# Nearest-neighbour upsampling: the first store cut into four transfers, and the closing waits moved to GpSimd

## The chip, the cores and the metric

The kernel runs on one core of one Trainium2 chip. The metric is the device time of one execution in microseconds (us), lower being better. Each comparison below was timed in rounds on one chip, with the kernel before in the same rounds. Kernels are compared only within the same rounds. A profiled execution comes with each; its "span", from the first to the last instruction, is about 1.8 us shorter than the device time. Unless said otherwise, times inside an execution count from the start of the span.

## The reference

The input is float32 of shape 16 x 64 x 64 x 64, and every element is repeated twice in height and twice in width. The loops of the reference come down to this:

```python
for i in range(new_h):
    for j in range(new_w):
        result[:, :, i, j] = x[:, :, i // 2, j // 2]
```

So 16.8 MB are read and 67.1 MB written, and nothing is computed.

## The kernel before

Four blocks of input are loaded, 4.2 MB each. VectorE and ScalarE expand rows inside SBUF, 9/16 and 7/16 of each piece, and SyncE issues all loads and stores on one queue. One input row is 256 B, and it becomes 1 KB of output. The two halves of one buffer take turns for eight stores of 32 rows for each partition ("small"), then two larger buffers for four stores of 64 rows ("large").

```python
blocks = [(1, M4, 0), (1, M4, 2), (1, M4, 3), (4, M4 // 4, 1)]   # the last load has rows of 8 KB, the others of 32 KB
for n, (j, m, slot) in enumerate(blocks):
    ...
    nc.sync.dma_start(out=..., in_=...)                            # all four loads, at the start

def store(part, r0, k, at):
    xp, first, m = part
    kv = k * 9 // 16
    ...
    nc.vector.tensor_copy(out=u[:, :kv], in_=expanded(xp[:, r0 : r0 + kv, :]))
    nc.scalar.copy(out=u[:, kv:], in_=expanded(xp[:, r0 + kv : r0 + k, :]))
    dst = of[first : first + P * m, :].rearrange("(p m) w -> p m w", p=P)
    nc.sync.dma_start(out=dst[:, r0 : r0 + k, :], in_=u)

for n, (q, r0) in enumerate(small):
    store(q, r0, 32, WX + n % 2 * (WU // 2))
for n, (q, r0) in enumerate(large):
    store(q, r0, 64, (0, WX)[n % 2])
```

A hook that the kernel already had issues the first load ahead of the opening barrier. Behind the kernel's own code stands a closing part that the framework adds. A semaphore is a counter on which transfers and engines report that they are done. SyncE waits for all eight DMA completion semaphores (called lanes here) and for VectorE and ScalarE. A barrier over all engines follows, GpSimd clears the semaphores, and a second barrier follows. In a barrier, GpSimd gathers one signal from each other engine and then releases them. "Drain" is an instruction in an engine's queue that here carries some of these waits and signals.

Of the kernel before, what the change touches and what calls it, by code (L numbers as in the profile page):

```python
# [1 line left out]

# [4 lines left out]



EARLY = 1  # L10


def begin_before_barrier(nc):



    blocks = nc.main_func.blocks
    main, body = blocks[0], blocks[1]
    sp = mybir.EngineType.SP
    loads = [i for i in body.instructions if i.engine == sp][:EARLY]  # L20
    for load in loads:
        assert isinstance(load, mybir.InstDMACopy), type(load)
        assert not (load.sync_info and load.sync_info.on_wait)
    names = [i.name for i in loads]
    body.instructions = [i for i in body.instructions if i.name not in names]
    kept = list(main.instructions)
    at = next(
        n
        for n, i in enumerate(kept)
        if i.engine == sp and isinstance(i, mybir.InstDrain)  # L30
    )
    kept[at:at] = loads
    main.instructions = kept


@with_exitstack
def kernel(
    ctx: ExitStack,
    tc: tile.TileContext,
    x: bass.AP,  # L40
    scale_factor: int,
    out: bass.AP,
):
    nc = tc.nc
    nc.at_finalize(begin_before_barrier)
    P = nc.NUM_PARTITIONS
    s = int(scale_factor)
    B, C, H, W = x.shape
    R = B * C * H
    fdt = x.dtype  # L50



    WX = R // P * W
    WU = 16384
    mem_pool = ctx.enter_context(tc.tile_pool(name="mem", bufs=1))
    mem = mem_pool.tile([P, WX + WU], fdt, name="mem")



    M4 = R // (4 * P)
    blocks = [(1, M4, 0), (1, M4, 2), (1, M4, 3), (4, M4 // 4, 1)]
    WB = M4 * W
    assert M4 * P * 4 == R and 2 * WB == WU

    xf = x.rearrange("b c h w -> (b c h) w")
    of = out.rearrange("b c (h hd) w -> (b c h) (hd w)", hd=s)

    parts = []
    for n, (j, m, slot) in enumerate(blocks):  # L70
        first = n * P * M4
        xt = mem[:, slot * WB : (slot + 1) * WB].rearrange(
            "p (j m w) -> p j m w", j=j, m=m
        )
        nc.sync.dma_start(
            out=xt.rearrange("p j m w -> p j (m w)"),
            in_=xf[first : first + P * M4, :].rearrange(
                "(j p m) w -> p j (m w)", j=j, p=P
            ),
        )  # L80
        parts.append([(xt[:, jj], first + jj * P * m, m) for jj in range(j)])

    def expanded(rows):
        return rows.unsqueeze(2).unsqueeze(4).to_broadcast(
            [P, rows.shape[1], s, W, s]
        )

    def store(part, r0, k, at):

        xp, first, m = part  # L90
        kv = k * 9 // 16
        u = mem[:, at : at + k * s * W * s].rearrange(
            "p (k a w b) -> p k a w b", k=k, a=s, w=W
        )
        nc.vector.tensor_copy(out=u[:, :kv], in_=expanded(xp[:, r0 : r0 + kv, :]))  # L95
        nc.scalar.copy(out=u[:, kv:], in_=expanded(xp[:, r0 + kv : r0 + k, :]))  # L96
        dst = of[first : first + P * m, :].rearrange("(p m) w -> p m w", p=P)
        nc.sync.dma_start(out=dst[:, r0 : r0 + k, :], in_=u)



    small = [(q, r0) for n in (0, 3) for q in parts[n] for r0 in range(0, q[2], 32)]
    large = [(q, r0) for n in (1, 2) for q in parts[n] for r0 in range(0, q[2], 64)]
    for n, (q, r0) in enumerate(small):
        store(q, r0, 32, WX + n % 2 * (WU // 2))
    for n, (q, r0) in enumerate(large):
        store(q, r0, 64, (0, WX)[n % 2])


# [1 line left out]
_INS = ['x', 'scale_factor']  # L111
_OUTS = [((16, 64, 128, 128), 'float32')]

_NUMBERS = {'scale_factor': 2}


# [26 lines left out]
```

## Time and profile before

| what | before |
|---|---|
| device time, median of 3 runs | 199.46 us |
| span of the profiled run | 197.7 us |
| first data packet starts, last one ends | 1.01 us, 196.58 us |
| last store landed, to the end of the span | 196.90 us, 0.81 us |
| VectorE, ScalarE busy | 20%, 26% |

These are lines of the page of the kernel before. The digits of the DMA row give the busy share of the 16 DMA engines in tenths, in 40 equal slices of the span. A packet is what one DMA engine moves at a time: 4 to 64 KB of data, or 4 bytes for a semaphore. In the last part the columns are the tensors, the issuing engine, the count, KB each (the page gives none for the four large stores) and the median us from issue to landing.

```profile
span 197.7 us, 116 instructions
DVE 40.2 (20%) x12; ACT 51.3 (26%) x13; POOL 0.2 (0%) x4
...
DMA  8999999999999999999999999999999999999994
...
DMA packets 2688, 83.89 MB, mean 424 GB/s; under 512 B 256, under 2 KB 256, under 8 KB 256
...
q1 hardware_dynamic: 2688, 83.89, 98.9%
...
out_dram<-mem SPq DMA_DIRECT2D x8, 4096.0 KB, 16.1
mem<-in_x_dram SPq DMA_DIRECT2D x4, 4096.0 KB, 25.8
out_dram<-mem SPq DMA_DIRECT2D x4, 32.3
```

The DMA row is full except for its first and last slice, so only three things can shorten this kernel: what stands ahead of the data, what stands behind it, and waste inside the full row.

The chain that ended last, in order of time (start us, us, what), starts so:

```profile
0.00 12.25 DMA mem<-in_x_dram
...
12.27 6.27 ACT mem L96 x2
...
18.56 43.03 DMA out_dram<-mem
```

ScalarE's 6.27 us seem to be on the critical path, but they are not: the other loads are moving all the while, as the DMA row shows. The 43.03 us run from the issue of the second store, at 18.56 us, to its landing at 61.58. The first store was issued at 15.5 us and landed at 51.9, for it stood behind the loads. The landings in the trace say so directly; this is computed from the semaphore records (us from the span's start, then the gaps):

```
loads        12.25  21.94  31.65  42.19                       gaps         9.69  9.71  10.54
small stores 51.90  61.58  71.24  80.92  90.61 100.28 ...     gaps  9.71   9.68  9.66 ...
large stores 138.98 158.31 177.60 196.90                      gaps 19.33  19.33 19.29  19.30
```

Everything lands every 9.7 us for 4.2 MB, except that the fourth load took 10.54 us.

The closing line of the kernel before, by engine queue and operation (count, then durations in ns as minimum, median and maximum, then first and last start in us):

```profile
L138 SPq EVENT_SEMAPHORE  x7: 17/28/28, 165.0 to 197.7; - x7
L138 POOLq EVENT_SEMAPHORE  x4: 17/17/17, 197.1 to 197.6; - x4
...
L138 SPq DRAIN  x3: 7/7/7, 197.0 to 197.3; - x3
...
L138 POOLq EVENT_SEMAPHORE_RANGE_CLEAR  x1: 93/93/93, 197.3 to 197.3; - x1
```

All four of GpSimd's semaphore instructions for the barriers stand behind the last landing at 196.90 us. So do both barriers, and none of it is hidden by data.

### The profile page before, as it was taken

What the parts mean: (1) busy time and instruction counts of PE and PEld (TensorE: products, weight loads), DVE (VectorE), ACT (ScalarE), POOL (GpSimd) and SP (SyncE); (2) the same over time, 40 slices, a digit from 0 to 9 for tenths busy, and PEclk for the clock granted to TensorE, in tenths of its full rate; (3) what the DMA queues carried; (4) which work ended last, traced back from release to release, by engine and by line L of the source; (5) the groups of instructions that cost most, each with busy time, mean ns of one, the idle gap of its engine ahead of it and who ended that gap; (6) DMA issues with size and microseconds to landing.
All of it is one profiled execution on the core that took longest, in us unless ns stands there. A gap on an engine that the chain in (4) does not pass through costs nothing.

```text
span 197.7 us, 116 instructions
## 1 busy us (share of the span) xinstructions
DVE 40.2 (20%) x12; ACT 51.3 (26%) x13; POOL 0.2 (0%) x4
## 2 busy tenths in 40 slices
DVE  0055000000405059505050007200810090000000
ACT  2057000000415150606069207400830092000000
POOL 0000000000000000000000000000000000000000
DMA  8999999999999999999999999999999999999994
GB/s 318 424 424 424 438 464 383 424 413 424 424 424 424 444 444 451 451 424 438 424 424 424 424 424 424 464 477 491 451 451 424 424 424 424 424 424 424 424 424 212
DMA packets 2688, 83.89 MB, mean 424 GB/s; under 512 B 256, under 2 KB 256, under 8 KB 256
## 3 DMA queue, kind: packets, MB, share of 16 engines
q1 hardware_dynamic: 2688, 83.89, 98.9%
HBM read 16.78 MB, written 67.11 MB: 424 GB/s over the span
## 4 chain that ended last, share of the span: by engine, by line
DMA 69%; ACT 14%; issue 0%; ACTq 0%
DMA out_dram<-mem 63%; ACT mem L96 14%; DMA mem<-in_x_dram 6%; ACTq L96 0%
## 5 line engine op out<-in xcount | busy, mean ns | idle before, releaser
L96 ACT COPY mem<-mem 128x3584 f32<-128x3584 f32 (+1 forms) x12 | 50.0, 4174 | 112.5 <-DMA out_dram<-mem 102.2
L95 DVE COPY mem<-mem 128x4608 f32<-128x4608 f32 (+1 forms) x12 | 40.2, 3359 | 123.1 <-DMA out_dram<-mem 110.8
L96 ACT ACT_TABLE_LOAD x1 | 1.3, 1283 | 0.8 <-PEq L124 0.8
L124 POOL MEMSET const-bfloat16-1.0<- 128x1 bf16 x1 | 0.1, 102 | 0.0
L124 POOL MEMSET const-uint8-127<- 128x1 uint8 x1 | 0.1, 102 | 0.0
L124 POOL MEMSET const-float32-0.0<- 128x1 f32 x1 | 0.1, 99 | 0.2 <-issue 0.2
L124 POOL MEMSET const-float32-1.0<- 128x1 f32 x1 | 0.1, 99 | 0.0
## 6 DMA issues: line engine op xcount, KB each, us to landing
out_dram<-mem SPq DMA_DIRECT2D x8, 4096.0 KB, 16.1
mem<-in_x_dram SPq DMA_DIRECT2D x4, 4096.0 KB, 25.8
out_dram<-mem SPq DMA_DIRECT2D x4, 32.3
```

The source lines that it names most:

```text
L95: nc.vector.tensor_copy(out=u[:, :kv], in_=expanded(xp[:, r0 : r0 + kv, :]))
L96: nc.scalar.copy(out=u[:, kv:], in_=expanded(xp[:, r0 + kv : r0 + k, :]))
L124: nc = _bacc.Bacc("TRN2", target_bir_lowering=False, num_devices=1)
```

## The change

One intent is to give the closing waits to GpSimd, which clears the semaphores itself. The first barrier, and the gather of the second, can then run while the last stores still move. After the last landing only a wait, the clear and the release remain. The wait for the last store is placed so that it stands alone and last.

The other intent, as far as the code tells, is to let the first store start with small pieces: 4, 4, 8 and 16 rows, of 4, 4, 8 and 16 KB for each partition. The first three need VectorE's copy alone.

```diff
+def close_on_gpsimd(nc):
+    ...
+    waits = sorted(wait.sync_info.on_wait, key=lambda w: w.id != last)
+    mine = [i for i in end if i.engine == pool]
+    ...
+    d0, gather0, release0, d1, clear, d2, gather1, release1 = mine
+    landed = mybir.InstDrain(name=wait.name, engine=pool, debug=wait.debug,
+        sync_info=mybir.SyncInfo(on_wait=waits, on_update=[]))
+    others = [i for i in end if i.engine != pool and i is not wait]
+    blocks[-1].instructions = others + [
+        d0, gather0, release0, gather1, d1, landed, clear, d2, release1
+    ]
...
     nc.at_finalize(begin_before_barrier)
+    nc.at_finalize(close_on_gpsimd)
...
-    def store(part, r0, k, at):
+    def store(part, r0, k, at, cuts=()):
...
-        nc.sync.dma_start(out=dst[:, r0 : r0 + k, :], in_=u)
+        cuts = (0, *cuts, k)
+        for lo, hi in zip(cuts, cuts[1:]):
+            nc.sync.dma_start(out=dst[:, r0 + lo : r0 + hi, :], in_=u[:, lo:hi])
...
-        store(q, r0, 32, WX + n % 2 * (WU // 2))
+        store(q, r0, 32, WX + n % 2 * (WU // 2), (4, 8, 16) if n == 0 else ())
```

More of the change, by code (lines that the diff above doesn't have):

```diff
@@ L33, in begin_before_barrier @@
     main.instructions = kept
+def close_on_gpsimd(nc):
+    blocks = nc.main_func.blocks
+    sp, pool = mybir.EngineType.SP, mybir.EngineType.Pool
+    stores = [
+        i
+        for i in blocks[1].instructions
+        if i.engine == sp and isinstance(i, mybir.InstDMACopy)
+    ]
+    last = stores[-1].sync_info.on_update[0].id
+    end = list(blocks[-1].instructions)
+    wait = end[0]
+    assert wait.engine == sp and isinstance(wait, mybir.InstDrain)
+    waits = sorted(wait.sync_info.on_wait, key=lambda w: w.id != last)
+    assert waits[0].id == last and len(waits) > 2
+    mine = [i for i in end if i.engine == pool]
+    kinds = [type(i).__name__ for i in mine]
+    assert kinds == [
+        "InstDrain",
+        "InstEventSemaphore",
+        "InstEventSemaphore",
+        "InstDrain",
+        "InstISA",
+        "InstDrain",
+        "InstEventSemaphore",
+        "InstEventSemaphore",
+    ], kinds
+    d0, gather0, release0, d1, clear, d2, gather1, release1 = mine
+    landed = mybir.InstDrain(
+        name=wait.name,
+        engine=pool,
+        debug=wait.debug,
+        sync_info=mybir.SyncInfo(on_wait=waits, on_update=[]),
+    )
+    others = [i for i in end if i.engine != pool and i is not wait]
+    blocks[-1].instructions = others + [
+        d0, gather0, release0, gather1, d1, landed, clear, d2, release1
+    ]
 @with_exitstack
```

## The prediction

> **What bounds the kernel now.** The DMA engines. The page gives DMA 9 or more in every slice but the first and last, one queue at 98.9% of 16 engines, VectorE 20% and ScalarE 26% busy. In the trace's packet records (times from the span's start) data moves without a gap from 1.0 to 196.6 us; a 32 KB packet takes 1213 ns on each of 16 engines, a 64 KB one 2418, an 8 KB one 309: about 27.2 B/ns plus 8 ns a packet. The chain of waits alternates DMA and ScalarE copies, which misleads: each copy lies under another transfer. The queue is served in order: the loads land at 12.3, 21.9, 31.6 and 42.2 us and the first store, ready at 15.5, at 51.9. The Trainium skill ("DMA: Bandwidth & Descriptors", Queues, rings and completion order) says that each engine consumes descriptors in ring order; these landings agree.
>
> Outside the data there is 1.0 us at the start, untouched, and 0.81 us at the end: from the last landing (196.9) to the end (197.7) SyncE's waits, a barrier, GpSimd's semaphore clear and a second barrier follow one another.
>
> One loss lies inside the stream. At the change from loads to stores each engine's last few 8 KB load packets take up to 0.9 us, not 309 ns; the last load takes 10.5 us against 9.7 for the same bytes elsewhere: 0.8 us lost.
>
> **What the change does.**
> 1. Earlier issue of the first pieces (they wait for VectorE alone): 0.6 us sooner on SyncE, worth nothing. They queue behind loads until about 41.5 us, 26 us after being ready.
> 2. More packets: three extra transfers, each 8 data packets and one semaphore packet per engine, at 8 to 9 ns: +0.2 us, critical, as the queue never empties. (Same page, Why small descriptors are slow: a fixed cost per packet; the trace's 8 ns agrees in kind.)
> 3. Smaller first packets may shorten the 0.8 us loss at the switch, as they stand beside the last loads. The trace doesn't say how much: I take 0.25 us saved, between 0 and 0.7.
> 4. Closing: the first barrier and the second gather are done before the last landing. After it remain GpSimd's drain that waits for the last store (that wait stands alone, last), the clear, a drain and the release. Before, GpSimd's drain to clear took 0.10 us, clear to second gather 0.20, gather 0.08, release to the end 0.10. So 0.81 becomes about 0.45: -0.37 us, all critical.
> 5. Completion lanes shift, but every store's extra wait is on a transfer landed long before. The first buffer is freed when all four pieces have landed, as late as before. The copies keep 6 us and more of slack.
>
> Sum: 199.46 + 0.2 - 0.25 - 0.37 = 199.0 us. Range 198.5 to 199.5. Faster by over 2%: 0.01; within 2%: 0.98; slower by over 2%: 0.01.
>
> **What would show it.** Step 1: the first pieces issued near 15 us, the last landing near 51.9 still. Step 2: 3,120 packets against 2,688, still no gap in the DMA slices. Step 3: the fourth load lands before 42.2 us, or does not. Step 4: 0.4 to 0.5 us from the last landing to the end; GpSimd, not SyncE, waits for the stores in the view of waits. Step 5: later stores land at the same spacing, 9.7 and 19.3 us.
>
> **What would make it wrong.** The loss at the switch vanishes (198.5 or below), or small store packets make it worse (199.5 and above); GpSimd sees the last store's semaphore later than SyncE did; or a closing part that the span doesn't show moves too.

## The result, and the profile after

The changed kernel took 199.20 us as a median of 6 runs (199.02 to 199.38), the kernel before 199.56 (199.43 to 199.73). The ratio is 0.9982, with a 95% interval of 0.9969 to 0.9995. The ratios here are from the runs of both kernels in the same rounds; they are not quite the ratios of the medians or of the means. The gain is 0.36 us, which is real but far below 2%.

The page after:

```profile
span 197.4 us, 119 instructions
DVE 40.2 (20%) x12; ACT 51.3 (26%) x13; POOL 0.2 (0%) x4
...
DMA  8999999999999999999999999999999999999994
...
DMA packets 3120, 83.89 MB, mean 425 GB/s; under 512 B 304, under 2 KB 304, under 8 KB 560
...
q1 hardware_dynamic: 3120, 83.89, 99.1%
...
out_dram<-mem SPq DMA_DIRECT2D x1, 2048.0 KB, 35.8
out_dram<-mem SPq DMA_DIRECT2D x2, 512.0 KB, 29.1
out_dram<-mem SPq DMA_DIRECT2D x1, 1024.0 KB, 31.5
```

The DMA row is as full as before with 432 more packets. The small pieces land some 30 us after they were issued, behind the loads: issuing them early gained nothing. The chain after:

```profile
0.00 12.18 DMA mem<-in_x_dram
...
12.21 6.27 ACT mem L142 x2
...
18.49 43.18 DMA out_dram<-mem
```

The stretch from the issue of the second store to its landing (61.67 us now) got longer, 43.18 us against 43.03. In the landings the fourth load still took 10.56 us (10.54 before), and the first store 9.83 us (9.71 before), in pieces of 1.27, 1.24, 2.45 and 4.87. The last store landed at 197.02 us instead of 196.90.

The closing line after:

```profile
L187 POOLq EVENT_SEMAPHORE  x9: 17/17/11952, 165.2 to 197.3; - x9
L187 POOLq DRAIN  x4: 34/38/70, 0.8 to 197.2; - x4
...
L187 SPq DRAIN  x2: 7/68/129, 165.1 to 165.4; - x2
L187 SPq EVENT_SEMAPHORE  x2: 17/17/17, 165.3 to 197.3; - x2
...
L187 POOLq EVENT_SEMAPHORE_RANGE_CLEAR  x1: 93/93/93, 197.1 to 197.1; - x1
```

GpSimd now starts its barrier work at 165.2 us. It is GpSimd that sits in a wait for a store (11,952 ns), and SyncE's drains are over at 165.4. What is left behind the last landing, from the instruction records (start in us):

```
before: last landing 196.90                    after: last landing 197.02
SyncE   last pair of waits      196.916        GpSimd drain, waits last store  197.039
SyncE   drain (waits ScalarE)   196.981        GpSimd clear                    197.103
SyncE   drain (signals)         197.039        GpSimd drain                    197.224
GpSimd  gather 1                197.071        GpSimd release                  197.288
GpSimd  release 1               197.149        TensorE's wait, ends            197.393
GpSimd  drain                   197.230
GpSimd  clear                   197.329
GpSimd  drain                   197.451
GpSimd  gather 2                197.529
GpSimd  release 2               197.607
TensorE's wait, ends            197.712
```

That is 0.81 us before and 0.37 after. In the two profiled runs the closing gave back 0.44 us, and the stream of data took 0.12 us longer. The sum, 0.32, is the difference of the two spans (197.71 and 197.39).

### The profile page after: what moved, and what is told of

Read it like the earlier page. It is cut to its first block, busy times and chain, and to the rows that moved or that the text cites. A ratio compares the mean times of both kernels' runs of the same rounds, so it can differ in the third digit from the quotient of the medians.

```text
span 197.4 us, 119 instructions
## 1 busy us (share of the span) xinstructions
DVE 40.2 (20%) x12; ACT 51.3 (26%) x13; POOL 0.2 (0%) x4
## 2 busy tenths in 40 slices
DMA packets 3120, 83.89 MB, mean 425 GB/s; under 512 B 304, under 2 KB 304, under 8 KB 560
## 3 DMA queue, kind: packets, MB, share of 16 engines
q1 hardware_dynamic: 3120, 83.89, 99.1%
## 4 chain that ended last, share of the span: by engine, by line
DMA 69%; ACT 14%; issue 0%; ACTq 0%
DMA out_dram<-mem 63%; ACT mem L142 14%; DMA mem<-in_x_dram 6%; ACTq L142 0%
```

## The experiments

The theory was that the closing gives the whole gain and the split only costs. The rival was that the split gives a part of the gain, by softening the loss at the switch from loads to stores. Eleven runs were made; each is an edit of the kernel before unless said otherwise.

### 1. The closing alone

```diff
-        store(q, r0, 32, WX + n % 2 * (WU // 2), (4, 8, 16) if n == 0 else ())     # of the changed kernel
+        store(q, r0, 32, WX + n % 2 * (WU // 2), ())
```

> The closing part alone, the first store whole. Theory A (the closing gives the whole gain of the change, the split costs a little): last landing to end 0.37 us instead of 0.81, last landing at 196.9 us, total 0.40 to 0.50 us below the kernel before, that is faster than the whole change by about 0.1. Rival B (the split gave part of the gain, by softening the switch from loads to stores): 0.1 to 0.25 us below the kernel before, slower than the whole change.

Measured: 199.00 us against 199.49 (5 and 9 runs), ratio 0.9977 (0.9965 to 0.9990). The last store landed at 196.96 us and 0.38 us remained. The means differ by 0.48 us, which is more than the whole change gained in its own rounds (0.36). This speaks for the theory, though the intervals of the two ratios overlap; experiments 10 and 11 compare the two side by side.

### 2. The split alone

```diff
-    nc.at_finalize(close_on_gpsimd)     # of the changed kernel
```

> The split of the first store alone, closing as before. Theory A: 0.1 to 0.2 us slower than the kernel before, last landing near 197.0 us, 0.81 us from there to the end. Rival B: 0.1 to 0.25 us faster than the kernel before, the fourth load landing earlier than 42.2 us.

Measured: 199.81 us against 199.49, ratio 1.0014 (1.0001 to 1.0026); the means differ by 0.25 us. The fourth load took 10.50 us, as in the runs with the first store whole (10.39 to 10.54). Slower, so the rival falls, but one part was not expected: the last store landed at 197.05 us, and 0.98 us followed instead of 0.81 (this time from the last landing to the end is called the tail below). The closing line shows why:

```profile
L186 SPq EVENT_SEMAPHORE  x7: 17/28/31936, 165.1 to 198.0; - x7
L186 POOLq EVENT_SEMAPHORE  x4: 17/17/17, 197.4 to 197.9; - x4
```

SyncE's ten closing waits are built as a list of instructions with up to two waits each. Before, the last store's lane stood in the last pair, and in first place. (In these traces a record starts when the first wait of its pair is fulfilled: in the kernel before, one starts at 177.615 us, just after the landing at 177.60 that stands first in it. So only a wait in second place shows as a duration; that is why the list of before had none over 28 ns.) With three more transfers the last store falls on another lane, whose wait stands in an earlier pair: SyncE sat there for 31,936 ns. After it, three more pairs still had to be gone through, at 197.107, 197.171 and 197.233 us, some 0.06 us each although all of them were long fulfilled.

### 3. The same cuts on the second store

```diff
-        store(q, r0, 32, WX + n % 2 * (WU // 2), (4, 8, 16) if n == 0 else ())     # of experiment 2
+        store(q, r0, 32, WX + n % 2 * (WU // 2), (4, 8, 16) if n == 1 else ())
```

> The same cuts on the second store instead of the first, away from the switch from loads to stores, closing as before. If the extra packets simply cost their 8 to 9 ns each (24 data packets and 3 semaphore packets per engine), 0.2 us slower, the second store's landing 9.9 us after the first's. If at the switch part of that cost is recovered, this run is slower than the split of the first store by about 0.1 us. If packets cost nothing in a full stream: no difference to before.

Measured: 199.86 us against 199.49, ratio 1.0018 (1.0004 to 1.0031). The cut store took 9.80 us (pieces of 1.24, 1.25, 2.45 and 4.86) where a whole one took 9.69, and the tail was 0.98 us again. So a split costs 0.11 to 0.13 us wherever it stands, not 0.2, and being next to the switch recovers nothing that can be told apart.

### 4. All eight small stores cut

```diff
-        store(q, r0, 32, WX + n % 2 * (WU // 2), (4, 8, 16) if n == 0 else ())     # of experiment 2
+        store(q, r0, 32, WX + n % 2 * (WU // 2), (4, 8, 16))
```

> All eight small stores cut in 4, 4, 8 and 16 rows, closing as before: the cost of the extra packets eight times over. If every packet costs 8 to 9 ns: +1.7 us to +1.8 us, 201.3 us, small stores landing 9.9 us apart instead of 9.7. If the extra packets are free in a full stream: no difference (within 0.2 us). If the extra semaphore packets or the splitting of the issue add waits of their own: over +2 us, with gaps in the DMA rows.

Measured: 200.57 us against 199.49, ratio 1.0055 (1.0043 to 1.0068); the means differ by 1.08 us, and the tail is 0.81 us again, as 24 more transfers bring the last store back to the old lane. From its page:

```profile
DMA packets 6144, 83.89 MB, mean 422 GB/s; under 512 B 640, under 2 KB 640, under 8 KB 2688
...
out_dram<-mem SPq DMA_DIRECT2D x16, 512.0 KB, 9.2
```

So 0.13 us for each cut store, eight times: linear, not free, and well under the 1.7 us expected. The reason lies in how packet records are read. The durations of packets overlap a little, so the cost of a packet is the distance from its start to the next start on the same engine (medians of the traces of the kernel before, the changed one and this one; the packed trace does not number the engines, so each packet is put behind the one that has just ended):

```
bytes     duration ns   start to start ns
4 (semaphore)   9             6
4,096         159           155
8,192         309           306
16,384        611           607
32,768       1213          1209
65,536       2418          2414
```

From 155 and 2414 ns the slope is 0.0368 ns for each byte, and 4.4 ns are left as the cost of a packet. A cut adds 24 data packets and 3 semaphore packets on each engine: 24 x 4.4 + 3 x 6 = 124 ns, which is what was measured. The Trainium skill ("DMA: Bandwidth & Descriptors", Why small descriptors are slow) gives a fixed overhead of about 3 cycles for each packet. At the 850 MHz that the page gives for the fabric, if that clock is meant, this would be 3.5 ns, which is an estimate; the trace's 4.4 ns are of that order.

### 5. The split alone, with SyncE's waits reordered

```diff
+    blocks[-1].instructions = [          # of the changed kernel, instead of moving the waits to GpSimd
+        mybir.InstDrain(name=wait.name, engine=sp, debug=wait.debug,
+            sync_info=mybir.SyncInfo(on_wait=waits, on_update=[]))    # the last store's wait alone and last
+    ] + end[1:]
```

> The split of the first store, the closing left on SyncE with both barriers, but SyncE's closing waits reordered so that the last store's wait stands alone and last. Theory: the split alone was 0.3 us slower for two reasons, 0.13 us of packets and 0.17 us because the three extra transfers move the last store to another completion lane, whose wait comes third from last in SyncE's list instead of last. Then this run has 0.75 us from the last landing to the end (0.98 in the split alone, 0.81 before) and is only about 0.1 us slower than before. Rival: the 0.17 us are chance or belong to the split's traffic, then they stay: 0.9 us or more, and +0.3 us in total.

Measured: 199.53 us against 199.56, ratio 1.0000 (0.9987 to 1.0012). The last store landed at 196.99 us and 0.75 us followed, as the theory of the lane says. The closing line of this run has the wait for the last store no longer in SyncE's pairs: the longest there, 12,627 ns, is for an earlier one.

```profile
L172 SPq EVENT_SEMAPHORE  x7: 17/28/12627, 165.0 to 197.7; - x7
```

The order of waits made the 0.23 us between 0.98 and 0.75. The 0.1 us that the packets should still have cost in total are not to be told from the scatter here.

### 6. The closing alone, with the second gather left behind the clear

```diff
-        d0, gather0, release0, gather1, d1, landed, clear, d2, release1     # of experiment 1
+        d0, gather0, release0, d1, landed, clear, d2, gather1, release1
```

> The closing alone as in the change, but with GpSimd's second gather left behind the clear, where it stood. Theory: that step costs 0.08 us of the chain and nothing more, so 0.45 us from last landing to end (0.38 with the early gather) and 0.37 us below the kernel before; the rest of the gain is the first barrier and SyncE's two drains taken off the end. Rival: the early second gather is what gives most of it, then 0.6 us and more.

Measured: 199.07 us against 199.56, ratio 0.9981 (0.9967 to 0.9994); 0.47 us from the last landing to the end, against 0.38 in experiment 1. The early gather is worth 0.09 us. The other 0.34 us (0.81 to 0.47) come from the first barrier, SyncE's drains and the order of the waits.

### 7. The last load in rows of 32 KB

```diff
-    blocks = [(1, M4, 0), (1, M4, 2), (1, M4, 3), (4, M4 // 4, 1)]
+    blocks = [(1, M4, 0), (1, M4, 2), (1, M4, 3), (1, M4, 1)]
```

> The kernel before with the last load in 32 KB rows instead of 8 KB rows (24 packets fewer on each engine, and the last packets before the switch four times as large). If the 0.7 us lost at the switch belong to a fixed amount of work in flight: same loss, total 0.1 us faster, fourth load in 10.4 us. If the loss is one of 8 KB packets beside large ones: fourth load 9.7 us, total 0.8 us faster. If the loss grows with the size of the last packets: slower, by up to 2 us.

Measured: 199.63 us against 199.56, ratio 1.0003 (0.9990 to 1.0015), the fourth load in 10.50 us. The loss at the switch is the same, with 32 KB packets: now mostly the last one of each engine is slow, 1741 to 2104 ns instead of 1213. Together with experiment 2 this says that the size of the packets, on either side of the switch, makes no difference that can be told from the scatter of the fourth load (10.39 to 10.56 us). The 0.1 us that 24 packets fewer on each engine should have saved does not show either; the interval of the ratio is about 0.25 us to either side.

### 8. The first store issued ahead of the last load

```diff
+        if n < 3:
+            load()
...
         store(q, r0, 32, WX + n % 2 * (WU // 2))
+        if n == 0:
+            load()                          # the fourth load
```

> The kernel before with the first store issued ahead of the last load, so that the queue changes from loads to stores twice and from stores to loads once. If each change from loads to stores loses 0.7 us: +0.7 us, the third load in 10.4 us instead of 9.7, and the fourth load's packets slowed at their end as before. If the loss happens once, or the change back gives as much: no difference. The copies keep their slack, as the first store is ready at 15.5 us and the third load lands at 31.6 us.

Measured: 200.08 us against 199.56, ratio 1.0025 (1.0012 to 1.0037). The third load, now the last before a store, took 10.87 us, the first store 9.90 and the fourth load 9.89. So neither expectation held as written: changing direction more often costs about 0.5 us, but it is not 0.7 us for each change from loads to stores. The first such change lost 1.2 us and the second about 0.1. The second change tells more. The second store had stood in the queue behind the fourth load since 18.64 us, and yet 506 of that load's 512 packets took 309 to 321 ns (the other six 338 to 571), and its 9.89 us are what it takes with no store behind it (9.91, experiment 9). So a store queued behind a load is not enough for the loss: here it fell on the first change from loads to stores alone. Why is left open. (The profiled execution was the slowest of the five, at 200.31 us, so these gaps are a little on the high side.)

### 9. The loads with no store queued behind them

```diff
-    small = [(q, r0) for n in (0, 3) for q in parts[n] for r0 in range(0, q[2], 32)]
+    small = [(q, r0) for n in (3, 0) for q in parts[n] for r0 in range(0, q[2], 32)]
```

> A diagnosis, slower on purpose: the small stores begin with the block that is loaded last, so that no store stands in the queue while loads run. If the 0.8 us at the switch come from stores queued behind the last loads (the engines read ahead into them): the fourth load takes 9.8 us or less and its last packets 309 ns. If they belong to the end of the loads: 10.5 us as before, with the same long packets. The total is some 4 us longer, as the queue is empty while the first copy runs.

Measured: 204.26 us (one run, state unknown; a diagnosis, not a candidate). The fourth load took 9.91 us, and its last packets 309 to 321 ns. So without stores queued behind the loads 0.5 to 0.65 us of the loss at the switch (10.39 to 10.56 us elsewhere) are gone. They did not move to the first store, whose packets took 1211 to 1253 ns, against 1213. In this one run the loss thus needs queued stores, while experiment 8 shows that they are not enough. That the engines read ahead into the stores was not shown, and it alone would not say why the second change was free. The rest, about 0.2 us, belongs to the load itself: by the table above, its 24 additional packets account for 0.1 us.

### 10 and 11. The change and the closing alone, side by side

The two kernels of the first comparisons, unchanged, on one chip in the same rounds.

> The changed kernel once more, to stand on the same chip beside the closing alone. 0.3 to 0.4 us below the kernel before; last landing near 197.0 us, 0.37 us from there to the end.

> The closing alone, on the same chip as the changed kernel. If the split costs its 0.12 us of packets and gives nothing back: 0.1 to 0.15 us faster than the changed kernel, 0.4 to 0.5 below the kernel before. Rival: with the closing on GpSimd the split is neutral, then both are equal within 0.05 us.

Measured: the change 199.13 us (199.08 to 199.29), the closing alone 199.08 us (199.01 to 199.22), the kernel before 199.52; ratios 0.9982 and 0.9978, each with an interval of about 0.0013 to either side. The means differ by 0.07 us in favour of the closing alone. The times of the two overlap, so these runs alone do not rank them; experiment 1 points the same way, and the traces show where the split costs (first store 9.82 us against 9.67 us, tail 0.38 us in both). The rival of "equal within 0.05 us" is not excluded by the times.

## Why the prediction was right or wrong

The predicted 199.0 us and the measured 199.2 agree within the range of 198.5 to 199.5, and "within 2%" was right. The terms of the sum, one by one:

- **The bound.** Right. The DMA row stayed full, and the time moved by what was added to the stream of data and taken from its tail.
- **Step 1, earlier issue worth nothing.** Right. The pieces left SyncE from 14.8 us on, and the last of them landed at 52.0.
- **Step 2, +0.2 us for more packets.** Right in kind, too large: it is 0.12 us. The term was built from packet durations of 8 to 9 ns over the data time; start to start a packet costs 4.4 ns. Experiment 4 shows it eightfold. The count of 3,120 packets was right.
- **Step 3, -0.25 us at the switch.** Wrong: nothing was saved, the low end of the 0 to 0.7 us that the prediction allowed. The fourth load took 10.42 to 10.56 us with the split and 10.39 to 10.54 with the first store whole. The prediction took it that smaller packets beside the last loads would disturb them less; experiments 2 and 7 show no effect of the packet sizes. Experiment 9 shows the loss gone when no store is queued behind the loads, but in experiment 8 a queued store did no harm at the second change. So what causes the loss stays open.
- **Step 4, -0.37 us for the closing.** Right in mechanism, a little small: 0.81 became 0.37 to 0.38 us, so it gave 0.44. The prediction charged 0.10 us from the drain to the clear, as before; the new drain that waits takes 0.06. The prediction feared that a closing part outside the span might move too. None did: device time less span is 1.79 us in both profiled runs. The prediction had said that the view of waits would name GpSimd's wait. It does not; the listing of the closing line does. In that view (who waited for what: us in total, times, longest us) SyncE waited for the stores before:

```profile
SPq L138 <- DMA out_dram<-mem: 31.8, 2, 19.3
```

After, it waits for the barrier instead, which the view puts down to the TensorE's queue (PEq), whose signal came last:

```profile
SPq L187 <- PEq L187: 32.1, 2, 31.9
```

- **Step 5, lanes without effect.** Right for the changed kernel, but the reason given covers only half of it. The stores do keep their spacing of 9.7 and 19.3 us. But the lane of the last store decides how many waits follow its own in the closing list. With the old closing the split would have cost 0.17 us more at the end; the new closing, which puts that wait last whatever its lane, hides this. The prediction's step 4 counted on that wait standing alone and last, but its step 5 looked at lanes between stores and not at the end.

Steps 2 and 3 nearly cancelled in the forecast (-0.05 us together), while they were +0.12 in the chip. That, less the 0.07 us that the closing gave beyond its term, leaves about 0.1 of the distance to 199.0; the rest is that the kernel before itself was at 199.56 in these rounds.

That the sum came so close is in part luck. Step 3 promised 0.25 us that did not come, and steps 2 and 4 were together 0.15 us too cautious. Nor does the range of 198.5 to 199.5 test much, as the kernel before, at 199.46 us, lies in it too. The steps are tested by the traces and the experiments alone.

## What to carry to other kernels

Where the DMA row is full from end to end, ask first what stands behind the last landing: here a third of a microsecond and more came from doing barriers while the last stores still moved, and from placing the wait that is fulfilled last at the end of its list. Cutting one transfer into several gave nothing here, as nothing waited for the first piece; in this full queue it cost a fixed amount for each packet, and that amount is to be read from start to start, not from durations. Undo the parts of a change one at a time: the better kernel was, as far as the traces tell, the one with only half of it.

## What the Trainium skill lacked or had wrong

- "DMA: Bandwidth & Descriptors", Anatomy of one DMA, gives a fixed cost of about 2.0 us for each DMA, and its Bandwidth section asks for 1 MiB and more (both measured on another issuing path). In a full queue neither binds: a further transfer costs 0.04 us (three of them 0.12), and 512 KB pieces landed every 1.25 us, which is 419 GB/s (524,288 B / 1.25 us).
- The same page gives the per-packet overhead in cycles, but does not say that recorded packet durations overlap: 8 ns by durations, 4.4 ns from start to start.
- No page consulted has the loss where a queue changes from loads to stores: 10.4 to 10.6 us for a load that takes 9.9 with no store behind it, with no effect seen of the packet size (8 or 32 KB in the load, 4 or 32 KB in the store). A second such change in the same execution did not have it (9.9 us, experiment 8).
- "Runtime: NRT & Kernel Launch", The ~15 us preamble/postamble breakdown, lists what the runtime adds. It does not list the kernel's own closing: 0.81 us from the last landing to the end of the span here, 0.38 us when most of it is done early.
- No page consulted says that a long list of waits is worked off in pairs at some 0.06 us a pair even when all are fulfilled, so that its order counts (0.98 against 0.75 us).
